# Inverting the triangular system of a gated delta rule: blocks of 32 solved on VectorE in place of blocks of 16 joined by products

## Chip, core and metric

The kernel runs on one core of a Trainium2 chip. The metric is the device time of one execution in microseconds (us). The core has TensorE (PE, with its weight loads shown as PEld), VectorE (DVE), ScalarE (ACT) and GpSimd (POOL); SyncE (SP) issues nearly all DMAs, in order, from one queue.

## The reference

The program is a whole small network on 256 tokens of width 1024: two layers of one kind (three sorts of attention), a norm, and then two layers of another kind (a mixer and a feed-forward). The change touches the mixer, and in it one branch, the chunked gated delta rule (4 heads, chunks of 64 tokens, key and value width 128). Cut to what matters:

```python
m = where(strict, einsum('bhnid,bhnjd->bhnij', k_beta, k) * decay, 0.0)
a = m + eye(64)                                    # unit lower triangular
rhs = concatenate([v * beta, k_beta * exp(G)])
u, w = split(triangular_solve(a, rhs))             # for each head and chunk
for each chunk:                                    # in order
    v_new = u - w @ state
    o     = q_dec @ state + attn @ v_new
    state = state * decay_last + k_tail.T @ v_new
```

Two tiles of 128 tokens hold four chunks; with 4 heads there are 8 matrices of 128x128, each with two triangular blocks of 64 on its diagonal. The mixer also has a retention branch, a pooling branch, gates, and three products (one for each branch) that are added up to `y`, which the output projection `w_out_2` takes.

## The kernel before

All large products are done as three fp32r products: weights are loaded from HBM as pieces of 128x1024 (512 KB) into `raw` (4 buffers); ACT casts a piece to `whi` and DVE subtracts to get `wlo` (7 buffers each); PE multiplies `whi` and `wlo` with the high and low parts of the activations (`xh`, `xl`) into `acc` (3 banks). Small products go to `sd` (5 banks) and are mostly plain fp32, which the trace shows as two records each.

The program is written down in one order, and each instruction is recorded with its inputs and outputs. A planner (`schedule`) then plays the five engines with estimated costs, always giving an engine the earliest recorded instruction that is ready, and hands out buffers of a class (`b` has 12 buffers of 4 KB per partition, `s` has 8) first come, first served in the order of the tiles. The order that comes out is what each engine executes. A dependency is seen by box: a slice of a rearranged view counts as the whole view, so two transfers into different slices of such a view follow one another in the plan.

In the mixer the inverse of each triangular block is built like this (`M` is the strict triangle, per tile `tt` and head `h`):

1. The products are masked to blocks of 16 (`m16`), and DVE folds each 128x128 to 128x16 (`tensor_reduce`, into `cN`, once for each `tt`). Eight transfers on SP's queue (8 KB each) bring one block to each of 64 partitions (`Nb`).
2. Substitution: 15 steps of two DVE instructions (a product into `tmp`, a subtraction from `Tb`) on 64 partitions, each step needing the one before. Step `j` has (15-j)(j+1) elements a partition.
3. Eight transfers bring the result back (`cT`), DVE spreads it to block diagonal form (`Tm`) and transposes it (`Sm`).
4. `level4` joins pairs of 16-blocks to 32-blocks: for each `tt` four PE products of `M` with `Sm`, a DVE mask (`mask4`), four PE products with `Tm`, a DVE subtraction from `Sm`, and DVE copies the 32-blocks to `Te`.
5. `level5` joins pairs of 32-blocks to 64-blocks with smaller products (recorded as 128*64 and 64*64).
6. `Sm` then gives `uu` and `wq`, and the loop over four chunks (the scan) runs through PE, ACT and DVE; its output `oTd` goes into the product with `w_branch_dn_2`, whose result is the last part of `y`.

The dense work that the text of the program puts around it, and that can fill PE while the chain of steps 1 to 6 waits, is: gate products, the branch products of pooling and retention, and the projections of v and q (`qkv`). The last dense work that does not need the scan's result is the two gate products `gate(0, h)`.

Of the kernel before, what the change touches and what calls it, by code (L numbers as in the profile page):

```python
# [13 lines left out]
ALU = mybir.AluOpType  # L14
# [29 lines left out]
def constants():  # L44
    t = np.arange(S)
    rc, rs = rope_np(t // 64, 32)
    cc, cs = rope_np(t % 64, 32)
    cosA, sinA = np.concatenate([rc, cc], 1), np.concatenate([rs, cs], 1)
    cosB, sinB = rope_np(t, 64)
    cosC, sinC = rope_np(t, 32)  # L50
    i = np.arange(P)
    ident = np.eye(P)
    m0 = np.where(i[None, :] <= i[:, None], 0.0, -1e30)
    mT0 = np.where(i[None, :] >= i[:, None], 0.0, -1e30)
    c1 = [ident, tok(cosA), tok(sinA), tok(cosB), tok(sinB), tok(cosC), tok(sinC), m0, mT0]
    same = (i[:, None] // 64) == (i[None, :] // 64)
    lt1 = (same & (i[:, None] <= i[None, :])).astype(float)
    ls = (same & (i[:, None] > i[None, :])).astype(float)
    r0 = np.repeat((i[:, None] < 64).astype(float), P, 1)
    r1 = 1.0 - r0  # L60
    masks = [((i[:, None] // 16) == (i[None, :] // 16)).astype(float)]
    for lv in range(4, 5):
        b = 2 ** lv
        masks.append((((i[:, None] // (2 * b)) == (i[None, :] // (2 * b)))
                      & ((i[None, :] // b) % 2 == 1) & ((i[:, None] // b) % 2 == 0)).astype(float))
    cosR, sinR = rope_np(t, 128)
    eye16 = np.tile(np.eye(16).reshape(1, 256), (P, 1))
    c2 = [lt1, ls, r0, r1, lt1.T] + masks + [tok(cosR), tok(sinR), eye16]
    gam = 1.0 - 2.0 ** (-5.0 - np.arange(4))
    jj, ii = t[:, None], t[None, :]  # L70
    ex = np.where((jj // 64) == (ii // 64), np.abs(ii - jj), ii - jj)
    dd = [np.where((jj // 64) <= (ii // 64), g ** np.maximum(ex, 0).astype(float), 0.0) * 128 ** -0.5 for g in gam]
    pc = []
    for w in (2, 4, 8, 16):
        pc.append(((jj <= ii) & (jj > ii - w)) / np.minimum(ii + 1.0, w) - (jj == ii))
    d0 = np.concatenate([a[:P] for a in dd], 1)
    d1 = np.concatenate([a[P:, P:] for a in dd], 1)
    p0 = np.concatenate([a[:P, :P + 16] for a in pc], 1)
    p1 = np.concatenate([a[P:, P:] for a in pc], 1)
    f = lambda l: np.ascontiguousarray(np.concatenate(l, 1).astype(np.float32))  # L80
    return {"k1": f(c1), "k2": f(c2), "kd0": f([d0]), "kd1": f([d1]), "kp0": f([p0]), "kp1": f([p1])}
# [313 lines left out]
class Net:  # L395
# [524 lines left out]


    def setup2(self):
        k2 = self.const("kk", [P, 1664], self.I["k2"])
        m = lambda i: k2[:, i * P:i * P + P]
        self.lt1, self.ls, self.r0, self.r1, self.li, self.m16 = (m(i) for i in range(6))
        self.mask4 = m(6)
        self.cosR = k2[:, 896:1152].rearrange("p (t d) -> p t d", t=2)
        self.sinR = k2[:, 1152:1408].rearrange("p (t d) -> p t d", t=2)
        self.eye16 = k2[:, 1408:1664].rearrange("p (r c) -> p r c", r=16)
        self.ones = self.nc.tile("c", [P, P])  # L930
        self.nc.vector.memset(self.ones, 1.0)
        self.lt1r = self.nc.tile("c", [P, P], F32R)
        self.nc.scalar.copy(self.lt1r, self.lt1)
# [4 lines left out]
    def mixer(self, l, xT, rx, nxt):  # L938
# [269 lines left out]

        y = [self.b(12 + tt, [P, D]) for tt in range(2)]
        branch("w_branch_pool_2", 0, oT, 0, gate(1, 0), True)  # L1210
        cp = self.b(0, [P, 832])
        cN, cT = (cp[:, i * P:i * P + P].rearrange("p (t h c) -> p t h c", t=2, h=4) for i in range(2))
        Nb, Tb = (cp[0:64, 320 + i * 256:576 + i * 256].rearrange("p (r c) -> p r c", r=16) for i in range(2))
        for tt in range(2):
            d16 = self.s2([P, 4, P])
            nc.vector.tensor_tensor(d16, M[:, tt], self.hb(self.m16), ALU.mult)
            nc.vector.tensor_reduce(cN[:, tt], d16.rearrange("p h (b c) -> p h c b", c=16), AX.X, ALU.add)
            for h in range(4):
                nc.sync.dma_start(Nb[(tt * 4 + h) * 8:(tt * 4 + h) * 8 + 8], cN[:, tt, h])
        nc.vector.tensor_copy(Tb, self.eye16[0:64])  # L1220
        for j in range(15):
            r, c = 15 - j, j + 1
            tmp = cp[0:64, 256:256 + r * c].rearrange("p (r c) -> p r c", r=r)
            nc.vector.tensor_tensor(tmp, Nb[:, c:16, j:j + 1].to_broadcast([64, r, c]),
                                    Tb[:, j:j + 1, 0:c].to_broadcast([64, r, c]), ALU.mult)
            nc.vector.tensor_tensor(Tb[:, c:16, 0:c], Tb[:, c:16, 0:c], tmp, ALU.subtract)
        for tt in range(2):
            for h in range(4):
                nc.sync.dma_start(cT[:, tt, h], Tb[(tt * 4 + h) * 8:(tt * 4 + h) * 8 + 8])
        Tm, Sm = self.b(8, [P, 2, 4, P]), self.b(9, [P, 2, 4, P])  # L1230
        for tt in range(2):
            nc.vector.tensor_tensor(Tm[:, tt].rearrange("p h (b c) -> p h b c", c=16),
                                    cT[:, tt].unsqueeze(2).to_broadcast([P, 4, 8, 16]),
                                    self.m16.rearrange("p (b c) -> p b c", c=16).unsqueeze(1).to_broadcast([P, 4, 8, 16]),
                                    ALU.mult)
            nc.vector.transpose(Sm[:, tt].rearrange("p h d -> p (h d)"), Tm[:, tt].rearrange("p h d -> p (h d)"))

        Te = [self.s2([64, 4, 64]) for tt in range(2)]

        def level4():  # L1240
            for tt in range(2):
                ps = self.sd([P, 4, P])
                for h in range(4):
                    nc.tensor.matmul(ps[:, h], M[:, tt, h], Sm[:, tt, h], start=True, stop=True)
                wt = self.s2([P, 4, P])
                nc.vector.tensor_tensor(wt, ps, self.hb(self.mask4), ALU.mult)
                ps = self.sd([P, 4, P])
                for h in range(4):
                    nc.tensor.matmul(ps[:, h], Tm[:, tt, h], wt[:, h], start=True, stop=True)
                nc.vector.tensor_tensor(Sm[:, tt], Sm[:, tt], ps, ALU.subtract)  # L1250
                for c in (0, 32):
                    nc.vector.transpose(Te[tt][c:c + 32, :, c:c + 32], Sm[2 * c:2 * c + 32, tt, :, 2 * c:2 * c + 32])
                    nc.gpsimd.memset(Te[tt][c:c + 32, :, 32 - c:64 - c], 0.0)

        def level5():
            v = lambda t: t.rearrange("p (c o r) -> p c o r", c=2, o=2)
# [22 lines left out]
        for tt in range(2):  # L1279
            nc.vector.tensor_tensor(kb[:, tt], kn[:, tt], hd(bGr, tt), ALU.mult)  # L1280
        branch("w_branch_ret_2", 0, oT, 4, gate(2, 0), False)
        level4()
        qkv(0, qT)
        rqs = []
        for tt in range(2):
# [219 lines left out]
```

## Time and profile before

| | us |
|---|---|
| median of 3 runs | 1184.65 (1184.16 to 1184.99) |
| profiled execution | 1186.84 |
| its span, first to last instruction | 1185.1 |
| PE busy in the span | 1167.3 |
| DVE busy | 875.3 |
| ACT busy | 651.0 |
| POOL busy | 48.2 |

Busy time is the union of an engine's instructions. The span is what the rows of the trace add up to; the profiled execution is 1.74 us longer than its span and 2.19 us longer than the median. The granted TensorE clock is 0.995 of full speed (2.4 GHz) over the span. Every instruction is recorded by one helper line (L392), so rows are told apart by engine, tile names and shapes. The two mixers are in the stretches around 200 to 520 us and 675 to 970 us.

### The profile page before, as it was taken

To read this page: it belongs to the slowest core of one execution; us is meant where nothing else is said; L and a number is where in the kernel's file an instruction comes from. 1 tells how busy PE (TensorE), PEld (TensorE's weight loads), DVE (VectorE), ACT (ScalarE), POOL (GpSimd) and SP (SyncE) were. 2 spreads that over 40 slices of the span, in tenths; PEclk is the share of its full clock that TensorE was granted. 3 is DMA by queue.
4 is the path that set the end of the run, shared out by engine and by line. 5 is a ranking of instruction groups with operands and counts; after the bars stand their busy time and mean duration, and the time that the engine had idled before them with its cause. 6 is when DMAs were issued, how large, how long until landed. Compare 5 with 4: busy or idle time off the path is not lost.

```text
span 1185.1 us, 17288 instructions
## 1 busy us (share of the span) xinstructions
PE 1167.3 (99%) x6316; PEld 989.9 (84%) x6316; DVE 875.3 (74%) x1549; ACT 651.0 (55%) x1209; POOL 48.2 (4%) x69
## 2 busy tenths in 40 slices
PE   8999999999999999999999999999999999999997
PEld 6888899888898888788888888898888878888886
DVE  5899789997698886776565638679797777655642
ACT  5689678965365554465454436445545446544531
POOL 0100010000001000000000001000000101000000
PEclk8999999999999999999999999999999999999999
DMA  6445345635464663345544854545654354654651
GB/s 235 137 145 167 122 130 175 194 128 174 119 212 144 210 203 128 103 160 198 209 156 136 273 194 142 170 141 169 220 186 152 107 178 140 202 192 142 214 195 36
DMA packets 64661, 196.67 MB, mean 166 GB/s; under 512 B 11200, under 2 KB 12352, under 8 KB 64576
## 3 DMA queue, kind: packets, MB, share of 16 engines
q1 hardware_dynamic: 64144, 195.10, 50.7%
q8 instruction: 49, 0.80, 0.3%
q10 hardware_dynamic: 432, 0.47, 0.1%
q14 instruction: 36, 0.29, 0.1%
HBM read 194.23 MB, written 1.05 MB: 165 GB/s over the span
## 4 chain that ended last, share of the span: by engine, by line
PE 92%; DVE 4%; ACT 2%; issue 1%; DMA 1%; ACTq 0%; POOLq 0%; DVEq 0%
PE acc L392 74%; PE sd L392 18%; DVE wlo L392 1%; DVE s L392 1%; DVE b L392 1%; DMA raw<-in_wt 1%; ACT whi L392 1%; ACT tg L392 0%; ACT s L392 0%; ACT b L392 0%; ACT xh L392 0%; DVE ty L392 0%; DVE m L392 0%; DVE tg L392 0%; DVE x L392 0%
## 5 line engine op out<-in xcount | busy, mean ns | idle before, releaser
L392 DVE TENSOR_TENSOR wlo<-raw,whi 128x1024 fp32r<-128x1024 f32 (+4 forms) x380 | 427.2, 1136 | 129.0 <-ACT whi L392 126.9
L392 ACT CAST whi<-raw 128x1024 fp32r<-128x1024 f32 (+4 forms) x379 | 368.2, 983 | 195.1 <-PE acc L392 140.7
L392 PE MATMUL acc<-whi,xh 128*128 128x512 f32 (+4 forms) x1184 | 446.1, 379 | 4.4 <-DVE ty L392 2.5
L392 PE MATMUL acc<-wlo,xh 128*128 128x512 f32 (+4 forms) x1184 | 442.9, 376 | 0.4 <-DVE wlo L392 0.4
L392 PE MATMUL acc<-whi,xl 128*128 128x512 f32 (+4 forms) x1184 | 442.9, 376 | 0.0
L392 PEld LDWEIGHTS acc<-whi,xh 128*128 128x128 f32 x1184 | 223.1, 189 | 42.7 <-ACT whi L392 3.3
L392 PEld LDWEIGHTS acc<-whi,xl 128*128 128x128 f32 x1184 | 223.5, 189 | 37.8 <-issue 0.4
L392 PEld LDWEIGHTS acc<-wlo,xh 128*128 128x128 f32 x1184 | 223.6, 189 | 37.7 <-DVE wlo L392 0.9
L392 PE MATMUL acc<-whi,b 128*128 128x512 f32 x328 | 107.4, 396 | 0.8 <-ACT b L392 0.8
L392 PEld LDWEIGHTS acc<-whi,b 128*128 128x128 f32 x328 | 61.5, 188 | 14.6 <-ACT b L392 1.1
L392 PE MATMUL sd<-b,b 128*128 128x128 f32 (+3 forms) x464 | 70.3, 289 | 0.0
L392 POOL TENSOR_TENSOR ty<-ty,m 128x4 f32<-128x4 f32 (+3 forms) x34 | 33.8, 997 | 886.3 <-DVE ty L392 886.3
L392 PE MATMUL acc<-wlo,b 128*128 128x512 f32 x164 | 64.5, 393 | 0.0
L392 PEld LDWEIGHTS sd<-b,b 128*128 128x128 f32 (+2 forms) x464 | 60.8, 190 | 4.3 <-DVE b L392 1.7
L392 ACT ACTIVATE b<-sd 128x512 fp32r<-128x512 f32 (+3 forms) x44 | 23.7, 538 | 64.7 <-PE sd L392 63.8
L392 ACT ACTIVATE s<-acc,r 128x512 f32<-128x512 f32 (+3 forms) x52 | 31.3, 601 | 49.1 <-PE acc L392 43.5
L392 PE MATMUL acc<-xh,wlo 128*128 128x256 f32 x192 | 53.9, 281 | 0.0
L392 PE MATMUL acc<-xh,whi 128*128 128x256 f32 x192 | 53.9, 281 | 0.0
L392 PE MATMUL acc<-xl,whi 128*128 128x256 f32 x192 | 53.8, 280 | 0.0
L392 DVE SCALAR_TENSOR_TENSOR b<-sd,b 128x512 fp32r<-128x512 f32 (+3 forms) x44 | 27.0, 616 | 18.7 <-ACT b L392 18.0
L392 PE MATMUL sd<-c,s 128*128 128x128 f32 (+2 forms) x236 | 36.7, 272 | 1.6 <-DVE s L392 1.6
L392 ACT ACTIVATE tg<-acc,r 128x512 f32<-128x512 f32 x24 | 16.5, 687 | 36.6 <-PE acc L392 36.6
(177 smaller groups left out, 1296.2 us busy)
## 6 DMA issues: line engine op xcount, KB each, us to landing
raw<-in_wt SPq DMA_DIRECT2D x308, 512.0 KB
raw<-in_wt SPq DMA_DIRECT2D x40, 256.0 KB
raw<-in_wt SPq DMA_DIRECT2D x16, 384.0 KB
b<-in_gains SPq DMA_DIRECT2D x5, 512.0 KB
raw<-in_wt SPq DMA_DIRECT2D x7, 352.0 KB
raw<-in_wt SPq DMA_DIRECT2D x8, 264.0 KB
b<-in_kd SPq DMA_DIRECT2D x2, 512.0 KB
kk<-in_k SPq DMA_DIRECT2D x1, 832.0 KB
```

The costliest lines, as they stand in the source:

```text
L392: o.inst = getattr(eng[o.eng], o.name)(*[real(a) for a in o.args], **{k: real(v) for k, v in o.kw.items()})
```

## The change

Masking, folding and substitution go by blocks of 32. The masks `m16` and `mask4` and the table `eye16` leave the constant `k2`, which shrinks from 1664 to 1280 columns; `m32` comes in. `cN` is 128x32 per tile and head. The eight transfers now bring 32-blocks to 32 partitions, into a tile `Nb` of its own, and are written with slices that are taken before any rearranging. The substitution is done in place in `Nb`, in 30 steps of two DVE instructions on 32 partitions; step `j` (1 to 30) has (31-j)j elements a partition. GpSimd writes -1 on the diagonals first. `level4` with its products goes. In its place `joined()`, recorded after the first half of the retention branch's product (where `level4` stood), negates `Nb` on ACT, sends it back in eight transfers, spreads it (`Tm`, now of class `s`), transposes it into `Sm`, and fills `Te` by four ACT copies. Tile `Sm` is asked for later than `vb` and `kb`, where it was before them; `Te` is asked for in `joined()`.

```diff
-        cp = self.b(0, [P, 832])
-        cN, cT = (cp[:, i * P:i * P + P].rearrange("p (t h c) -> p t h c", t=2, h=4) for i in range(2))
-        Nb, Tb = (cp[0:64, 320 + i * 256:576 + i * 256].rearrange("p (r c) -> p r c", r=16) for i in range(2))
+        cp = self.b(0, [P, 768])
+        cN, cT = (cp[:, i * S:i * S + S].rearrange("p (t h c) -> p t h c", t=2, h=4) for i in range(2))
+        Nb = self.b(0, [32, 32, 32])
         for tt in range(2):
-            d16 = self.s2([P, 4, P])
-            nc.vector.tensor_tensor(d16, M[:, tt], self.hb(self.m16), ALU.mult)
-            nc.vector.tensor_reduce(cN[:, tt], d16.rearrange("p h (b c) -> p h c b", c=16), AX.X, ALU.add)
-            for h in range(4):
-                nc.sync.dma_start(Nb[(tt * 4 + h) * 8:(tt * 4 + h) * 8 + 8], cN[:, tt, h])
-        nc.vector.tensor_copy(Tb, self.eye16[0:64])
-        for j in range(15):
-            r, c = 15 - j, j + 1
-            tmp = cp[0:64, 256:256 + r * c].rearrange("p (r c) -> p r c", r=r)
-            nc.vector.tensor_tensor(tmp, Nb[:, c:16, j:j + 1].to_broadcast([64, r, c]),
-                                    Tb[:, j:j + 1, 0:c].to_broadcast([64, r, c]), ALU.mult)
-            nc.vector.tensor_tensor(Tb[:, c:16, 0:c], Tb[:, c:16, 0:c], tmp, ALU.subtract)
-        for tt in range(2):
-            for h in range(4):
-                nc.sync.dma_start(cT[:, tt, h], Tb[(tt * 4 + h) * 8:(tt * 4 + h) * 8 + 8])
-        Tm, Sm = self.b(8, [P, 2, 4, P]), self.b(9, [P, 2, 4, P])
...
-        def level4():
+            d32 = self.s2([P, 4, P])
+            nc.vector.tensor_tensor(d32, M[:, tt], self.hb(self.m32), ALU.mult)
+            nc.vector.tensor_reduce(cN[:, tt], d32.rearrange("p h (b c) -> p h c b", c=32), AX.X, ALU.add)
+            for h in range(4):
+                nc.sync.dma_start(Nb[(tt * 4 + h) * 4:(tt * 4 + h) * 4 + 4], cp[:, (tt * 4 + h) * 32:(tt * 4 + h) * 32 + 32])
+        nc.gpsimd.memset(Nb.rearrange("p r c -> p (r c)")[:, 0:1024:33], -1.0)
+        for j in range(1, 31):
+            r, c = 31 - j, j + 1
+            tmp = cp[0:32, 512:512 + r * j].rearrange("p (r c) -> p r c", r=r)
+            nc.vector.tensor_tensor(tmp, Nb[:, c:32, j:c].to_broadcast([32, r, j]),
+                                    Nb[:, j:c, 0:j].to_broadcast([32, r, j]), ALU.mult)
+            nc.vector.tensor_tensor(Nb[:, c:32, 0:j], Nb[:, c:32, 0:j], tmp, ALU.subtract)
+        def joined():
+            nc.scalar.activation(Nb, Nb, AF.Copy, scale=-1.0)
             for tt in range(2):
-                ps = self.sd([P, 4, P])
                 for h in range(4):
-                    nc.tensor.matmul(ps[:, h], M[:, tt, h], Sm[:, tt, h], start=True, stop=True)
-                wt = self.s2([P, 4, P])
-                nc.vector.tensor_tensor(wt, ps, self.hb(self.mask4), ALU.mult)
-                ps = self.sd([P, 4, P])
-                for h in range(4):
-                    nc.tensor.matmul(ps[:, h], Tm[:, tt, h], wt[:, h], start=True, stop=True)
-                nc.vector.tensor_tensor(Sm[:, tt], Sm[:, tt], ps, ALU.subtract)
+                    nc.sync.dma_start(cp[:, S + (tt * 4 + h) * 32:S + (tt * 4 + h) * 32 + 32],
+                                      Nb[(tt * 4 + h) * 4:(tt * 4 + h) * 4 + 4])
+            Sm = self.b(9, [P, 2, 4, P])
+            Te = [self.s2([64, 4, 64]) for tt in range(2)]
+            for tt in range(2):
+                Tm = self.s2([P, 4, P])
...
+                nc.vector.transpose(Sm[:, tt].rearrange("p h d -> p (h d)"), Tm.rearrange("p h d -> p (h d)"))
                 for c in (0, 32):
-                    nc.vector.transpose(Te[tt][c:c + 32, :, c:c + 32], Sm[2 * c:2 * c + 32, tt, :, 2 * c:2 * c + 32])
+                    nc.scalar.copy(Te[tt][c:c + 32, :, c:c + 32], cT[2 * c:2 * c + 32, tt])
                     nc.gpsimd.memset(Te[tt][c:c + 32, :, 32 - c:64 - c], 0.0)
+            return Sm, Te
...
-        level4()
+        Sm, Te = joined()
```

## Rows read from the trace of the kernel before

**Rows 1.** The page: the span, and busy time, share and instructions of each engine

```profile
span 1185.1 us, 17288 instructions
PE 1167.3 (99%) x6316; PEld 989.9 (84%) x6316; DVE 875.3 (74%) x1549; ACT 651.0 (55%) x1209; POOL 48.2 (4%) x69
```

**Rows 2.** The page: the chain that ended last, shares of the span by engine

```profile
PE 92%; DVE 4%; ACT 2%; issue 1%; DMA 1%; ACTq 0%; POOLq 0%; DVEq 0%
```

**Rows 3.** Stretches: length, then busy us (instructions) of each engine, clock, DMA share, GB/s

```profile
376.00:389.50 13.50, 13.50 (x68) 11.30 (x67) 10.31 (x11) 7.10 (x8) 0.00 (x0) 1.00 0.70 210
389.50:426.00 36.50, 36.50 (x241) 33.14 (x240) 31.28 (x65) 17.62 (x22) 0.00 (x0) 1.00 0.65 214
426.00:441.00 15.00, 15.00 (x75) 12.54 (x74) 13.21 (x21) 9.40 (x15) 0.00 (x0) 1.00 0.55 161
441.00:454.00 13.00, 13.00 (x57) 10.53 (x56) 7.11 (x8) 4.83 (x6) 0.00 (x0) 1.00 0.63 203
470.00:490.00 20.00, 19.18 (x123) 16.26 (x122) 12.66 (x22) 8.87 (x21) 1.01 (x1) 1.00 0.41 132
490.00:520.00 30.00, 28.80 (x134) 23.05 (x135) 20.81 (x31) 12.49 (x24) 1.01 (x1) 1.00 0.48 158
903.00:916.00 13.00, 13.00 (x57) 10.50 (x57) 9.43 (x13) 4.89 (x5) 0.00 (x0) 1.00 0.60 191
950.00:1000.00 50.00, 49.25 (x231) 39.63 (x230) 38.20 (x70) 27.05 (x55) 4.14 (x5) 1.00 0.50 164
```

**Rows 4.** Timeline of PE, both mixers: start, length, operation, records, idle before

```profile
456.13 2.01 PE L392 MATMUL sd<-b,b 128*128 128x128 f32 x16
457.89 0.48 PE L392 MATMUL acc<-wlo,xh 128*128 128x512 f32 x1
...
458.64 1.95 PE L392 MATMUL sd<-s,b 128*128 128x128 f32 x16
460.43 0.60 PE L392 MATMUL sd<-c,b 128*128 128x128 f32 x4
...
462.75 0.68 PE L392 MATMUL sd<-b,s 128*64 128x64 f32 x8
...
489.87 0.50 PE L392 MATMUL acc<-whi,b 128*128 128x512 f32 x1 [0.82 <-ACT b L392]
```

**Rows 5.** Timeline of SP's queue: the small transfers (b<-b)

```profile
376.34 0.80 SPq L392 DMA_DIRECT2D b<-b  x1
...
387.35 0.61 SPq L392 DMA_DIRECT2D b<-b  x1
...
401.81 0.61 SPq L392 DMA_DIRECT2D b<-b  x1
...
447.99 0.63 SPq L392 DMA_DIRECT2D b<-b  x1
...
909.54 0.63 SPq L392 DMA_DIRECT2D b<-b  x1
```

**Rows 6.** Timeline of DVE in the two mixers

```profile
391.04 1.05 DVE L392 TENSOR_REDUCE b<-s 128x64 f32<-128x512 f32 x1
...
406.66 0.59 DVE L392 TENSOR_TENSOR b<-b 64x15 f32<-64x15 f32 x3
...
414.82 0.21 DVE L392 TENSOR_TENSOR b<-b 64x60 f32<-64x60 f32 x1
414.95 0.68 DVE L392 TENSOR_TENSOR b<-b,tg 128x512 f32<-128x512 f32 x1
...
421.83 1.80 DVE L392 TENSOR_TENSOR b<-b 64x55 f32<-64x55 f32 x8
...
454.12 1.29 DVE L392 TENSOR_TENSOR b<-b,kk 128x512 f32<-128x512 f32 x2
455.32 1.30 DVE L392 STREAM_TRANSPOSE b<-b 128x512 f32<-128x512 f32 x2
...
913.13 0.69 DVE L392 TENSOR_TENSOR b<-b,kk 128x512 f32<-128x512 f32 x1 [2.79 <-DMA raw<-in_wt]
```

**Rows 7.** Groups by shape: count, busy us, mean ns of one, idle before

```profile
L392 DVE TENSOR_TENSOR b<-b 64x63 f32<-64x63 f32 x8 | 1.7, 213 | 0.1
L392 DVE TENSOR_TENSOR b<-b 64x15 f32<-64x15 f32 x8 | 1.3, 168 | 0.2
L392 DVE STREAM_TRANSPOSE s<-b 32x128 f32<-32x128 f32 x8 | 2.4, 299 | 0.1
L392 ACT CAST whi<-raw 128x1024 fp32r<-128x1024 f32 x308 | 320.1, 1052 | 177.9 <-PE acc L392 124.4 <-DMA raw<-in_wt 22.8 <-PE sd L392 21.8
```

More of the change, by code (lines that the diff above doesn't have):

```diff
@@ L60, in constants @@
     r1 = 1.0 - r0
[L61 to L65, printed above, removed]
+    m32 = ((i[:, None] // 32) == (i[None, :] // 32)).astype(float)
     cosR, sinR = rope_np(t, 128)
-    eye16 = np.tile(np.eye(16).reshape(1, 256), (P, 1))
-    c2 = [lt1, ls, r0, r1, lt1.T] + masks + [tok(cosR), tok(sinR), eye16]
+    c2 = [lt1, ls, r0, r1, lt1.T, m32, tok(cosR), tok(sinR)]
     gam = 1.0 - 2.0 ** (-5.0 - np.arange(4))
@@ L922, in setup2 @@
     def setup2(self):
-        k2 = self.const("kk", [P, 1664], self.I["k2"])
+        k2 = self.const("kk", [P, 1280], self.I["k2"])
         m = lambda i: k2[:, i * P:i * P + P]
[L925 to L929, printed above, removed]
+        self.lt1, self.ls, self.r0, self.r1, self.li, self.m32 = (m(i) for i in range(6))
+        self.cosR = k2[:, 768:1024].rearrange("p (t d) -> p t d", t=2)
+        self.sinR = k2[:, 1024:1280].rearrange("p (t d) -> p t d", t=2)
         self.ones = self.nc.tile("c", [P, P])
@@ L1227, in mixer @@
-        for tt in range(2):
-            for h in range(4):
-                nc.sync.dma_start(cT[:, tt, h], Tb[(tt * 4 + h) * 8:(tt * 4 + h) * 8 + 8])
-        Tm, Sm = self.b(8, [P, 2, 4, P]), self.b(9, [P, 2, 4, P])
[L1231 to L1236, printed above, removed]
@@ L1238, in mixer @@
-        Te = [self.s2([64, 4, 64]) for tt in range(2)]
-        def level4():
+                nc.sync.dma_start(Nb[(tt * 4 + h) * 4:(tt * 4 + h) * 4 + 4], cp[:, (tt * 4 + h) * 32:(tt * 4 + h) * 32 + 32])
[6 more added lines that the diff above has]
+            nc.vector.tensor_tensor(Nb[:, c:32, 0:j], Nb[:, c:32, 0:j], tmp, ALU.subtract)
@@ L1250, in level4 @@
-                nc.vector.tensor_tensor(Sm[:, tt], Sm[:, tt], ps, ALU.subtract)
+                    nc.sync.dma_start(cp[:, S + (tt * 4 + h) * 32:S + (tt * 4 + h) * 32 + 32],
[4 more added lines that the diff above has]
+                Tm = self.s2([P, 4, P])
+                nc.vector.tensor_tensor(Tm.rearrange("p h (b c) -> p h b c", c=32),
+                                        cT[:, tt].unsqueeze(2).to_broadcast([P, 4, 4, 32]),
+                                        self.m32.rearrange("p (b c) -> p b c", c=32).unsqueeze(1).to_broadcast([P, 4, 4, 32]),
+                                        ALU.mult)
+                nc.vector.transpose(Sm[:, tt].rearrange("p h d -> p (h d)"), Tm.rearrange("p h d -> p (h d)"))
```

## The prediction

> **What bounds the kernel now.** I read the page first. PE is busy 1167.3 of 1185.1 us and holds 92% of the chain that ended last [rows 1, 2], so work taken from PE comes off the span if PE stays fed, and idle that the edit brings to PE goes on. Next I read the stretches around the edit. From 376 to 454 us PE has no idle at all, while DVE is busy 61.9 of 78 us, so DVE has 16.1 us to spare there [rows 3]. PE is idle 0.82 us in 470 to 490, 1.20 in 490 to 520, and in the second mixer 0.75 in 950 to 1000 [rows 3]. That small idle matters. The last timeline row of PE shows the first product of the branch that needs the scan (`acc<-whi,b`) starting at 489.87 after a wait for ACT's copy of the scan's result [rows 4]: the fillers ran out just as the scan ended. So two lines meet there, PE's total work and the chain from the fold of `M` through substitution, transfers, `level4`, `level5` and scan. A gain needs both to get shorter.
>
> The chain in the first mixer reads: first small transfer issued at 376.34, eighth at 401.81 [rows 5], substitution from 406.66 [rows 6] to about 425, last transfer back at 447.99 [rows 5], spreading at 454.12 and transposes from 455.32 [rows 6], `level4` on PE from 456.13, `level5` from 462.75 [rows 4]. From 455 on it is tight: the transposes of `Sm` and the first `level4` product overlap.
>
> **PE, the term of the sum.** `level4` is 16 fp32 products a mixer, 32 records. The first set holds PE from 456.13 to 457.89, 1.76 us; the second from 458.64 to 460.43, 1.79 us [rows 4]. That is 3.55 us a mixer, 7.1 us in all. Nothing is added on PE.
>
> **DVE.** The new substitution has 60 instructions in place of 30, with 2 x (sum of (31-j)j for j from 1 to 30) = 9920 elements in place of 1360. The rows give 168 ns for 15 elements and 213 for 63 [rows 7]: 0.94 ns an element. When another instruction follows, the next one starts 0.13 us after a product of 60 elements (414.82 to 414.95) [rows 6], so 0.074 us is fixed. When the chain runs alone, eight of mean 42.5 elements take 1.80 us [rows 6]: 0.225 each, 0.185 fixed. The new substitution therefore takes between 60 x 0.074 + 9.3 = 13.8 us and 60 x 0.185 + 9.3 = 20.4 us of DVE; the old one between 3.5 and 6.8. I expect some 40 of the 60 gaps of 0.11 us to be filled by other work, as in the rows of before, where products and casts alternate: 16 us. `level4` gives back two masks and two subtractions (0.6 us each from start to start) and four transposes of 0.30 us [rows 7]: 3.6 us. Net, DVE gets some 7 us a mixer; against 16.1 us to spare it fits, and the `wlo` casts stay covered because seven buffers are ahead of PE (ACT's casts wait mostly for PE to release one [rows 7]). Without that cover each late cast would stop PE for its lateness.
>
> Here a page of the Trainium skill speaks against the edit. VectorE: DVE Perf Modes (the section on the TRN2 errata) says that instructions from SBUF pay a fixed latency each, asks for 512 elements and more in one, and gives (N+151)/0.96 ns for an fp32 tensor_tensor. By it the 60 take 60 x 157 ns + 10.3 us = 19.8 us, as an estimate. The trace agrees with it for an instruction that stands alone (213 ns against 223 for 63 elements), not where another follows. By it the substitution would end near 450 and nearly nothing would be gained: the border between the first two rivals below.
>
> **The chain's new length.** I follow it in the first mixer.
> - Start. The first four transfers no longer follow one another: four issues of 0.62 us from 376.34. One landed 3.59 us after its issue began (909.54, and DVE's wait ends at 913.13) [rows 5, 6]. So `tt` 0 lands by 381.9. The second fold (1.05 us; it stood at 391.04, after the fourth transfer at 387.35) and four more transfers with two weight loads between them follow; the -1 on the diagonal is one short GpSimd instruction. Substitution starts near 389.5 instead of 406.66.
> - Substitution. From 389.5 to 426 DVE has 5.2 us idle [rows 3], plus the old substitution's 3.5 to 5.9 us and the old fold's 1.05: about 11 of the 16 to 16.4 us. The rest, about 20 instructions of 0.27 us, alternates with other instructions of 0.63 us (13.21 us for 21 [rows 3]): 18 us more, end at 444. Bounds: 436 if every gap is filled, 451 if none is.
> - Back. ACT's copy of 32x1024 costs at most the 1.05 us of a 128x1024 cast [rows 7], with a short wait 445.3. Eight issues of 0.62 us with two weight loads between: last issue near 450.3, landed at 453.9. Two spreads and two transposes, with `kb` ahead of them because `Sm` gets its buffer after it: `level5` can start near 457, bounds 449 and 464. It stood at 462.75.
>
> Two new waits have work queued behind them. DVE's first substitution step and its spreading wait for transfers, with `wlo` casts behind; at 910 to 913 DVE waited 2.79 us for such a transfer [rows 6] and PE had no idle from 903 to 916 [rows 3], so the seven prepared buffers cover that much. On SP's queue the eight returns wait for ACT's copy, with weight loads behind, as they waited for DVE's last step before; the same buffers cover it.
>
> The four ACT copies into `Te` (0.3 us each) lie in a stretch where ACT is busy 4.83 of 13 us [rows 3], and GpSimd is idle; both cost nothing. They would sit on the chain if they came after the transposes, at most 1.2 us. The shorter constant is 192 KB less once, at a time when PE is never short of weights: nothing.
>
> **The meeting point.** PE is 3.55 us ahead of before when `level4` is gone, so the whole gain needs `level5` at or ahead of 459.2 (substitution done by about 446); at 462.75 (substitution done by about 450) nothing is gained; later it costs. My 457 is inside by some 2 us. Then the scan ends 5.7 us earlier while PE is 3.55 earlier, so 2 us of fillers are left and part of the idle of 2.0 and 0.75 us goes too; I take 1 us of 2.75, because the waits at the end of the branch remain. Sum: 7.1 + 1.0 = 8.1 us. The profiled execution, 1186.84 us with span 1185.1, would become 1178.7, its span 1177; the median stands 2.19 us lower than the profiled execution, 1184.65, and becomes 1176.5.
>
> **Rivals.**
> - *DVE holds the substitution back.* Place: 389 to 450 us, where the substitution shares DVE with conv taps and `wlo`. For it: from 389.5 to 441 DVE is already 86% busy (44.5 of 51.5) [rows 3], and the chain cannot be hidden behind itself. Against: the substitution is recorded ahead of that work and so goes first whenever it is ready. It decides from an end at 450 on. At 451 and `level5` at 464 it costs 1.3 us a mixer past before, 1187; with 5 us more delay, 1197. Chance 13% of a loss over 0.2%.
> - *Part of the gain.* Substitution ends between 446 and 450; 0 to 7.1 us are left, 1178 to 1184. Chance 25%, 10 points of it within 0.2%.
> - *The transfers get slower.* They carry 128 pieces of 128 B where they had 64 B. If all of the 3 us between issue and landing doubled at the three places in the chain, `level5` comes 9 us later, at 466: 1184.65 + 2 x 3 = 1191. No row separates the time of the pieces from the fixed part. A rule of the Trainium skill makes it possible: DMA: Bandwidth & Descriptors (the section on why a DMA increments its semaphore by 16) has a transfer split over the largest number of engines that divides both slowest dimensions, which would be 4 here and was 8. No row here shows the engines of one transfer. Chance 4%, counted as slower by half.
> - *PE not the bound after all*, so that 3.55 us turn to waits elsewhere at once: 1184.65. Against: 92% of the chain is PE [rows 2]. Chance 3%.
>
> **Chances and range.** The full gain (1174.5 to 1178) has 55%; part of it, but over 0.2%, 15%; within 0.2% (2.4 us, about what a measurement of this kernel can tell from no change) 15%; slower 15%. The range reaches from 1174 (7.1 + 2.75 + the rounding of a record or two) to 1184.5, leaving out the losses and a few points of luck below. The likeliest case's own range is 1174.5 to 1178.
>
> **What would show it.** PE's records of `sd<-s,b 128x128` vanish and `sd<-b,b 128x128` fall by 32; PE's busy time falls by about 7 us and its idle does not grow. DVE shows 60 instructions on 32 partitions a mixer, from about 390 to 444, busy total up by some 14 us. The small transfers stand in groups of four and eight. `level5` (128*64) starts near 457 in the first mixer, with no PE wait ahead of it. I am wrong if PE shows idle of several us between 440 and 500 or `acc` products waiting for `wlo`; then the substitution's last instruction after 450 names the DVE rival, a long wait of the spreading instruction for a transfer the other.

## The result, and the profile after

| | before | after |
|---|---|---|
| median, both on one chip | 1184.82 us (1184.16 to 1186.09, 4 runs) | 1172.74 us (1172.02 to 1173.72, 4 runs) |
| profiled execution, its span | 1186.84, 1185.1 | 1172.4, 1170.6 |

The ratio is 0.9897, 95% interval 0.988 to 0.9914: the change gains 12.1 us where 8.1 were forecast, and 1172.74 lies 1.3 us below the range of 1174.0 to 1184.5. The sign was right, the size was not.

The page of the kernel after, its first lines (span, busy time of each engine) and the shares of the chain that ended last, which answer to [rows 1] and [rows 2]:

```profile
span 1170.6 us, 17214 instructions
PE 1155.2 (99%) x6252; PEld 980.1 (84%) x6252; DVE 886.7 (76%) x1591; ACT 653.5 (56%) x1219; POOL 49.3 (4%) x71
...
PE 85%; DVE 8%; ACT 3%; issue 2%; DMA 1%; SPq 1%; POOLq 0%; DVEq 0%; ACTq 0%
```

PE is busy 12.1 us less and its idle falls from 17.8 to 15.4 us (span less busy). That the 12.1 equals the gain of the medians is chance: 2.5 us of it lie ahead of the first mixer, for the reason below, and 9.6 behind. DVE does 11.4 us more. The chain's share of PE fell from 92 to 85%, and yet PE is idle less: the view follows one way back, and where two lines are both just in time it may as well take the one through DVE. The idle in the stretches, not the share, says what bounds.

The two profiled executions differ by 14.4 us, the medians by 12.1. The difference is in the beginning, which the change touches only by a smaller constant. Stretches of the kernel after and, below it, of the kernel before (columns as in [rows 3]):

```profile
20.00:40.00 20.00, 18.77 (x96) 15.06 (x97) 17.76 (x42) 12.77 (x27) 2.91 (x2) 1.00 0.53 158
```

```profile
20.00:40.00 20.00, 18.42 (x85) 14.40 (x84) 16.12 (x36) 13.30 (x27) 3.14 (x3) 0.91 0.47 145
```

The granted clock was 0.91 in these 20 us before, 1.00 after, and with it PE reaches the gate math of the first mixer (the products `sd<-m,kk`) at 346.39 before and 343.99 after. So the times of after that follow are 2.4 us early against those of before; the rows show no other reason, and all ten traces fit it (last section). From that mark to the same mark of the second mixer it is 461.55 us before and 454.75 after, from there to the end of the span 377.16 and 371.86: 6.8 and 5.3 us, together the 12.1.

The chain in the first mixer, after. SP's queue with the small transfers (`b<-b`), answering to [rows 5]:

```profile
373.65 2.57 SPq L387 DMA_DIRECT2D b<-b  x4
376.32 2.15 SPq L387 DMA_DIRECT2D raw<-in_wt  x4
379.14 2.47 SPq L387 DMA_DIRECT2D b<-b  x4
382.51 50.64 SPq L387 DMA_DIRECT2D raw<-in_wt  x17
435.30 5.21 SPq L387 DMA_DIRECT2D b<-b  x8
```

DVE's timeline, answering to [rows 6]:

```profile
378.03 1.08 DVE L387 TENSOR_REDUCE b<-s 128x128 f32<-128x512 f32 x1
...
386.86 0.19 DVE L387 TENSOR_TENSOR b<-b 32x30 f32<-32x30 f32 x1
387.08 0.20 DVE L387 TENSOR_TENSOR b<-b,b 32x30 f32<-32x30 f32 x1
...
402.24 0.47 DVE L387 SCALAR_TENSOR_TENSOR s<-s,pp,s 128x255 f32<-128x255 f32 x1
402.63 0.38 DVE L387 TENSOR_TENSOR b<-b,b 32x228 f32<-32x228 f32 x1
402.94 0.47 DVE L387 SCALAR_TENSOR_TENSOR s<-s,pp,s 128x255 f32<-128x255 f32 x1
403.33 0.38 DVE L387 TENSOR_TENSOR b<-b 32x234 f32<-32x234 f32 x1
...
433.96 0.17 DVE L387 TENSOR_TENSOR b<-b,b 32x30 f32<-32x30 f32 x1
...
442.80 1.29 DVE L387 TENSOR_TENSOR b<-b,m 128x512 f32<-128x512 f32 x2 [1.19 <-DMA b<-b]
444.01 1.29 DVE L387 TENSOR_TENSOR s<-b,kk 128x512 f32<-128x512 f32 x2
```

PE's timeline around `level5`, answering to [rows 4]:

```profile
433.86 0.60 PE L387 MATMUL sd<-c,b 128*128 128x128 f32 x4
...
446.61 1.15 PE L387 MATMUL sd<-b,s 128*64 128x64 f32 x16
...
449.20 1.11 PE L387 MATMUL sd<-s,s 64*64 64x64 f32 x16 [0.31 <-ACT s L387]
```

The stretches of [rows 3], shifted by 2.7 us; the columns are the same:

```profile
386.80:423.30 36.50, 36.50 (x242) 33.08 (x241) 36.02 (x80) 15.48 (x19) 0.00 (x0) 1.00 0.51 158
423.30:438.30 15.00, 15.00 (x82) 12.69 (x81) 14.96 (x36) 9.91 (x14) 0.00 (x0) 1.00 0.53 171
438.30:451.30 13.00, 12.69 (x84) 10.26 (x83) 10.79 (x24) 8.54 (x29) 1.98 (x2) 1.00 0.47 151
467.30:487.30 20.00, 20.00 (x101) 16.42 (x100) 16.47 (x24) 11.02 (x20) 2.02 (x2) 1.00 0.55 179
```

What to see: four transfers are issued in a row and no longer follow one another; substitution runs from 386.86 to 434.13, between `wlo` casts and conv taps (`s<-s,pp,s`), with DVE busy 36.02 of 36.50 us and then 14.96 of 15.00; PE does not notice, it has no idle until 438. The spreading (`s<-b,kk`) is at 444.01, and `level5` starts at 446.61 with no wait ahead of it, 102.6 us after the mark, where it was 116.4 before; a short wait of 0.31 us comes behind it. Around the end of the scan, where PE was idle 0.82 us before, it has no idle now. By shape, `sd<-b,b 128x128` has 208 records in place of 240 and `sd<-s,b`, 32 records before, is gone.

Both PE timelines, each product's time taken from its start to the start of the next, give the 12.1 us in three parts (idle is the waits of 0.15 us and more):

| | from the first mark to the second | from there to the end | sum | forecast |
|---|---|---|---|---|
| products of `level4` | 3.56 | 3.56 | 7.1 | 7.1 |
| PE idle | 1.70 | 0.65 | 2.35 | 1.0 |
| all other products, a little closer together | 1.5 | 1.1 | 2.6 | 0 |

The idle of before that matters lies in four waits around the end of the scan: the one at 489.87 [rows 4], here with the group ahead of it, and three more. The second fence is of after, where no wait is left at this place:

```profile
488.45 0.60 PE L392 MATMUL sd<-c,b 128*128 128x128 f32 x4
...
496.44 0.66 PE L392 MATMUL sd<-c,b 128*128 128x128 f32 x4 [0.35 <-DVE b L392]
497.95 0.47 PE L392 MATMUL acc<-whi,xh 128*128 128x512 f32 x1 [0.85 <-DVE tg L392]
...
957.98 0.47 PE L392 MATMUL acc<-whi,xh 128*128 128x512 f32 x1 [0.75 <-ACT b L392]
```

```profile
494.62 0.60 PE L387 MATMUL sd<-c,b 128*128 128x128 f32 x4
494.97 0.48 PE L387 MATMUL acc<-whi,xh 128*128 128x512 f32 x1
```

A wait costs more than the idle that the row names. Before, four records start at 488.45 and the next product at 489.87, 1.42 us later, of which 0.82 are idle; after, the next product starts 0.35 us behind the start of such a group. The wait of 0.82 us thus cost 1.07, because the last product ahead of a wait stands with its whole length and otherwise overlaps the next. The four waits, 2.77 us of idle, have about 0.25 us each of this, 1.0 us in all, and it stands in the third row of the table.

### The profile page after: what moved, and what is told of

It reads as the page before. It is cut to its first block, busy times and chain, and to the rows that moved or that the text cites. A ratio compares the mean times of both kernels' runs of the same rounds, so it can differ in the third digit from the quotient of the medians.

```text
span 1170.6 us, 17214 instructions
## 1 busy us (share of the span) xinstructions
PE 1155.2 (99%) x6252; PEld 980.1 (84%) x6252; DVE 886.7 (76%) x1591; ACT 653.5 (56%) x1219; POOL 49.3 (4%) x71
## 4 chain that ended last, share of the span: by engine, by line
PE 85%; DVE 8%; ACT 3%; issue 2%; DMA 1%; SPq 1%; POOLq 0%; DVEq 0%; ACTq 0%
PE acc L387 68%; PE sd L387 17%; DVE b L387 3%; DVE wlo L387 2%; DVE s L387 2%; DMA raw<-in_wt 1%; ACT whi L387 1%; ACT s L387 1%; ACT tg L387 1%; SPq L387 1%; DMA b<-b 0%; ACT b L387 0%; ACT xh L387 0%; DVE ty L387 0%; DVE xl L387 0%
## 5 line engine op out<-in xcount | busy, mean ns | idle before, releaser
L387 PE MATMUL sd<-b,b 128*128 128x128 f32 (+4 forms) x432 | 66.8, 290 | 0.0
L387 PEld LDWEIGHTS sd<-b,b 128*128 128x128 f32 (+2 forms) x432 | 57.1, 190 | 4.1 <-DVE b L387 1.3
```

The source lines that it names most:

```text
L387: o.inst = getattr(eng[o.eng], o.name)(*[real(a) for a in o.args], **{k: real(v) for k, v in o.kw.items()})
```

## The experiments

**The theory.** PE and the chain are two lines that meet at `level5` and at the end of the scan; the gain is PE's products plus the idle that the chain no longer causes, and after the change the chain has time to spare. Rivals: the transfers alone did it; the products did it alone and DVE's part is idle luck; or the chain is still what sets the end. Costs below are against the kernel after, from the difference of the two ratios times the 1184.65 us of before. "From the mark on" compares the traces behind the first mixer's `sd<-m,kk`, where the beginning no longer plays a part.

**The transfers alone.** The kernel before with slices taken ahead of any rearranging:

```diff
-                nc.sync.dma_start(Nb[(tt * 4 + h) * 8:(tt * 4 + h) * 8 + 8], cN[:, tt, h])
+                i = tt * 4 + h
+                nc.sync.dma_start(cp[i * 8:i * 8 + 8, 320:576].rearrange("p (r c) -> p r c", r=16), cp[:, i * 16:i * 16 + 16])
...
-                nc.sync.dma_start(cT[:, tt, h], Tb[(tt * 4 + h) * 8:(tt * 4 + h) * 8 + 8])
+                i = tt * 4 + h
+                nc.sync.dma_start(cp[:, P + i * 16:P + i * 16 + 16], cp[i * 8:i * 8 + 8, 576:832].rearrange("p (r c) -> p r c", r=16))
```

> The kernel before with one part of the change alone: the sixteen small transfers are written with slices taken before any rearranging, so the plan no longer sets them one behind the other. Blocks stay at 16, level4 and its products stay. Theory A (two lines: PE's work, and the chain that meets it at the end of the scan): the chain starts some 17 us earlier, PE's work is unchanged; what goes is PE's idle at the end of the scan (1.7 us in the first mixer, 0.65 in the second by the two traces) and the hidden waits of the small products (about 2.2 us in both): 1184.8 - 2.4 - (0 to 2.2) = 1180 to 1182.5. Theory B (the whole gain is work taken from PE): 1184.8, within 0.1%. Theory C (the chain's start, not the products, brought most of the 12 us): 1177 or lower.

Measured: 1181.67 us, ratio 0.9968 [0.9957, 0.998], 3.8 us off before. PE's timeline of this kernel, the first product of `level5`:

```profile
438.24 0.68 PE L392 MATMUL sd<-b,s 128*64 128x64 f32 x8
```

It stood at 462.75; against the mark it comes 22.3 us earlier. A chain so much shorter, with the same products on PE, is worth little more than the idle around the scan (2.75 us in the rows of before): PE's total then decides. From the mark on, the trace is 3.4 us shorter than that of before: 2.5 us of idle and the rest mostly what hung on the four waits. Theory A holds.

**The transfers undone.** The kernel after, with whole rearranged views as before:

```diff
-        Nb = self.b(0, [32, 32, 32])
+        Nb = self.b(0, [32, 1024]).rearrange("p (r c) -> p r c", r=32)
...
-                nc.sync.dma_start(Nb[(tt * 4 + h) * 4:(tt * 4 + h) * 4 + 4], cp[:, (tt * 4 + h) * 32:(tt * 4 + h) * 32 + 32])
+                nc.sync.dma_start(Nb[(tt * 4 + h) * 4:(tt * 4 + h) * 4 + 4], cN[:, tt, h])
...
-                    nc.sync.dma_start(cp[:, S + (tt * 4 + h) * 32:S + (tt * 4 + h) * 32 + 32],
+                    nc.sync.dma_start(cT[:, tt, h],
```

> The changed kernel with the small transfers written through rearranged views again, so that the plan sets them one behind the other; blocks of 32, no level4. Theory A: the fold of the second tile and the substitution start some 17 us later and the way back is some 15 us longer; level5, which stands at 449 on the clock of the trace before, moves to about 480, against 462.75 before; some 17 us a mixer late less 7 us of PE's lead is exposed, as far as no dense work can be pulled forward: 1172.7 + 2 x (10 to 20) = 1190 to 1212. Theory B: 1172.7, since PE's work is the same; up to 1176 with some idle. The rival of the prediction that DVE holds the chain back has the same sign as A here and is told apart by the run that doubles DVE's products.

Measured: 1226.17 us, ratio 1.0342 [1.0328, 1.0356]: 53 us over after and 3.4% slower than before. PE's timeline, `level5` in both mixers:

```profile
480.94 1.97 PE L387 MATMUL sd<-b,s 128*64 128x64 f32 x16 [12.12 <-DVE b L387]
...
963.54 1.97 PE L387 MATMUL sd<-b,s 128*64 128x64 f32 x16 [12.05 <-DVE b L387]
```

The same sixteen transfers a mixer that were worth 3.8 us with the short substitution are worth 53 with the long one, since most of the delay now lies past the chain's spare (see the detours below). The sign was expected, the size not: the waits of 12.1 us are only about half. The stretch that begins before the first of them shows the rest:

```profile
470.00:490.00 20.00, 9.06 (x56) 8.83 (x57) 7.79 (x14) 5.29 (x11) 0.52 (x1) 0.58 0.34 111
490.00:520.00 30.00, 23.99 (x118) 19.72 (x117) 14.93 (x29) 7.16 (x23) 2.02 (x2) 0.77 0.11 36
```

PE is busy 9.06 of 20 us and the granted clock is 0.58, so nearly all of this stretch is at the lower of the two levels, 1.2 GHz, and a part of the next 30 us still is. The 16 records of `level5` take 1.97 us where they take 1.15 after. From the mark of the first mixer to that of the second, idle grew by 17.8 us and the products, the same in number, took 9.8 us more from start to start.

**The products put back.** The kernel after, with as many products as `level4` had, in a block ahead of `joined()`; nothing reads their results:

```diff
+        for tt in range(2):
+            for n in range(2):
+                ps = self.sd([P, 4, P])
+                for h in range(4):
+                    nc.tensor.matmul(ps[:, h], M[:, tt, h], M[:, tt, h], start=True, stop=True)
         Sm, Te = joined()
```

> The changed kernel with 16 fp32 products of 128x128 a mixer (M with M, results read by nobody) recorded ahead of the joining step: PE's work of before without level4's place in the chain. Theory A: the price of the products alone, 7.1 us by the rows of before (7.6 by the difference of the two traces): 1172.7 + 7.1 to 7.6 = 1179.8 to 1180.4, with PE's idle as small as in the changed kernel. Theory B (all 12 us are the products and what hangs on them on PE): 1183 to 1185. Theory C: the products fill idle of PE, under 3 us: below 1175.7.

Measured: 1183.36 us, ratio 0.9988 [0.9977, 0.9999], 10.8 us over after, more than the products' own time and in theory B's interval. PE's timeline:

```profile
414.05 3.73 PE L387 MATMUL sd<-b 128*128 128x128 f32 x32
...
445.91 0.68 PE L387 MATMUL sd<-b,s 128*64 128x64 f32 x8 [0.62 <-ACT s L387]
```

The records take 3.5 us a mixer from start to start, 7.0 together. From the mark on the trace is 10.3 us longer than that of after: these 7.0, 1.6 of new idle (most of it at `level5`, which now waits 0.62 and 0.99 us for ACT) and 1.7 in other products, 0.5 of them because `level5` runs as groups of 8 again. So the number falls in theory B's interval, but a third of it is not the products: it is waits and spacing that came with this plan.

**The same products, spread.** To see whether the block makes it dear, the same 16 were placed one at a time between the steps of a dense product (pooling, second half):

```diff
             self.mm3(ps, xh[:, k0 + k, s], xl[:, k0 + k, s], wh[:, k % KT], wl[:, k % KT], k == 0, k == nk - 1)
+            if getattr(self, "extra", None) and k < nk - 1:
+                self.extra.pop()()
...
+        def product(tt, h):
+            ps = self.sd([P, P])
+            nc.tensor.matmul(ps, M[:, tt, h], M[:, tt, h], start=True, stop=True)
+        self.extra = [lambda tt=tt, h=h: product(tt, h) for n in range(2) for tt in range(2) for h in range(4)]
         branch("w_branch_pool_2", 1, oT, 0, gate(1, 1), True)
```

> The changed kernel with 16 extra fp32 products a mixer, as in the run that had them in one block, now one at a time between the dense fp32r products of the gate and pooling branch. The block cost 10.6 us where its own records took 7.0. Theory A (a small fp32 group inside the dense stream costs more than its own records, 0.09 us and up for each return to dense products): some 13 more insertions a mixer cost 26 x 0.09 to 0.2 = 2.3 to 5.2 us on the products' own 7.1: 1182 to 1185. Theory B (insertions cost nothing; the block's 3.5 us extra were waits that it brought to the small products behind it): 1179.8 to 1180.5.

Measured: 1183.84 us (1180.59 to 1184.96, 12 runs), ratio 0.999 [0.998, 1.0]: 11 us over after, the same as the block. That the number falls in theory A's interval does not bear out its account, since spreading changed nothing, and theory B's lower figure was missed too. The profiled execution is 8.2 us over that of after, but it began with the clock at 1.00 and reached the mark 1.3 us sooner; from the mark on it is 9.5 us longer. Of these 4.9 are the products' records from start to start and 2.6 the dense product behind each insertion (0.32 us in place of 0.23), together 7.5 where the block took 7.0; 1.1 are new idle (0.91 and 0.74 us at `level5`, for ACT again) and the rest is spacing. So an insertion costs about 0.1 us, but its records take less (0.08 us each, 0.11 in the block), and spreading changes little.

**The chain later by one detour.** In `joined()`, a quarter of `Nb` makes a way out and back by two transfers that follow one another:

```diff
         def joined():
+            for n in range(1):
+                t = cp[0:32, 512:768].rearrange("p (r c) -> p r c", r=8)
+                nc.sync.dma_start(t, Nb[:, 0:8])
+                nc.sync.dma_start(Nb[:, 0:8], t)
             nc.scalar.activation(Nb, Nb, AF.Copy, scale=-1.0)
```

> The changed kernel with one detour in the chain: after the substitution a quarter of Nb is sent to a scratch area and back by two transfers that follow one another, some 7 us of waiting with no work on PE or DVE. Theory A: level5 goes from 449 to about 456 on the clock of the trace before; PE's line, which has lost 7 us of work and idle, would need it by 462.75 - 6.9 = 455.9: 1172.7 to 1174.7. Theory B (chain hidden): 1172.7. Theory C (chain binds in the changed kernel): 1172.7 + 2 x 7 = 1186.7.

Measured: 1173.04 us, ratio 0.9894 [0.9881, 0.9908]. `level5` came 6.5 us later in the first mixer and 7.2 in the second, both against the mark, and the time did not move. In the first mixer that is 455.5 on the clock of before, close to the 457 that the prediction had, and of the four waits around the scan only one of 0.25 us is there.

**By two detours.** The same with `range(2)`.

> The changed kernel with two detours in the chain (four transfers one behind the other after the substitution), some 14 us of waiting with no work on PE or DVE. One detour moved level5 from 449 to 456 on the clock of the trace before and cost nothing. Theory A (the chain has some 7 us to spare and then binds): level5 near 463, 7 us past the point where PE's line needs it; dense work pulled forward hides a part: 1172.7 + 2 x (1.5 to 7) = 1176 to 1187. Theory B (the chain is hidden whatever its length, and the boxed run lost its time elsewhere): 1172.7 to 1174.

Measured: 1188.54 us, ratio 1.0027 [1.0016, 1.0038]: 15.4 us over after, and 1.5 above theory A's interval. PE's timeline of the first mixer, with one detour and then with two:

```profile
453.24 0.68 PE L387 MATMUL sd<-b,s 128*64 128x64 f32 x8
```

```profile
459.92 0.68 PE L387 MATMUL sd<-b,s 128*64 128x64 f32 x8
...
463.65 0.65 PE L387 MATMUL sd<-s,s 64*64 64x64 f32 x8 [1.59 <-ACT s L387]
...
485.31 1.16 PE L387 MATMUL sd<-st,b 128*128 128x128 f32 x8 [2.15 <-DVE st L387]
```

Now `level5` is 14.4 and 15.0 us later than after and PE has waits at each step of the chain behind it. The first 7 us were free, the next 7 to 8 cost 15.4 in both mixers together, about one to one if the spare ends at 7, which no run shows more closely than between 7 and 14. It is an average: from the first mark to the second this trace is 11.4 us longer than that of after, from there to the end 3.4. In the first mixer the waits brought the clock down:

```profile
466.00:470.00 4.00, 4.00 (x23) 4.00 (x23) 0.00 (x0) 0.96 (x2) 0.00 (x0) 0.57 0.27 102
470.00:486.00 16.00, 13.18 (x86) 11.05 (x85) 11.81 (x18) 7.98 (x17) 2.05 (x1) 1.00 0.55 169
486.00:494.00 8.00, 6.97 (x27) 5.78 (x26) 4.24 (x9) 2.19 (x9) 0.68 (x1) 0.57 0.15 58
```

There the products took 6.1 us more beside 5.3 of idle; in the second mixer, where the clock stayed at 1.00, only 0.7 more. The twelve executions took from 1184.4 to 1190.2 us, and this trace is of one 2.4 us below the median. The run with whole views fits the average too: there `level5` is 32.7 and 35.1 us later, 25.7 and 28.1 past a spare of 7, together 53.8, and 53 were measured. Theory B falls here, and with one detour the rival by which the chain still sets the end in the kernel after.

**The substitution's DVE work.** Its product is done twice, into the same `tmp`:

```diff
+            nc.vector.tensor_tensor(tmp, Nb[:, c:32, j:c].to_broadcast([32, r, j]),
+                                    Nb[:, j:c, 0:j].to_broadcast([32, r, j]), ALU.mult)
             nc.vector.tensor_tensor(Nb[:, c:32, 0:j], Nb[:, c:32, 0:j], tmp, ALU.subtract)
```

> The changed kernel with each product of the substitution done twice into the same scratch (30 more DVE instructions a mixer, same results): 6.9 to 10.2 us more DVE work in the chain and in the stretch where DVE is fullest. Theory A (only the chain's end counts, and it has 7 us to spare): level5 comes 7 to 10 us later, 456 to 459 on the clock of the trace before: 1172.7 to 1178. The prediction's rival (DVE short of time, so that wlo casts come late and PE starves): over 1180, with PE's dense products waiting for wlo in the trace.

Measured: 1201.68 us, ratio 1.014 [1.0126, 1.0154]: 28.8 us over after for 30 short instructions a mixer. Theory A falls for this step, the DVE rival came. DVE's timeline (the last instruction of the substitution), PE's, and the stretches:

```profile
456.83 0.18 DVE L387 TENSOR_TENSOR b<-b,b 32x30 f32<-32x30 f32 x1
```

```profile
447.62 0.50 PE L387 MATMUL acc<-whi,xh 128*128 128x512 f32 x1 [2.21 <-DVE tg L387]
...
451.35 0.79 PE L387 MATMUL acc<-wlo,xh 128*128 128x512 f32 x1 [3.23 <-DVE wlo L387]
...
469.75 0.68 PE L387 MATMUL sd<-b,s 128*64 128x64 f32 x8
```

```profile
390.00:426.00 36.00, 36.00 (x235) 32.52 (x234) 35.56 (x78) 14.98 (x20) 0.00 (x0) 1.00 0.51 163
426.00:441.00 15.00, 14.88 (x77) 12.14 (x76) 15.00 (x37) 9.21 (x20) 0.00 (x0) 1.00 0.36 113
441.00:454.00 13.00, 7.56 (x27) 5.57 (x26) 11.84 (x30) 3.55 (x13) 1.98 (x2) 0.78 0.27 92
```

DVE was full already, so 30 more instructions end the substitution 22.9 us later and push `wlo` and the retention's `tg` behind them; PE, whose cover lasted to 441, then waits for both, and the clock of that stretch is 0.78. `level5` is 23.2 and 24.2 us later than after. Of PE's waits over 0.3 us in the chain's stretch of both mixers, 8.2 us are for `tg` and `wlo`, ahead of `level5`, and 7.3 for the chain behind it. Both mechanisms are there, and the run does not separate their costs.

**The products and masks of `level4` taken away.** The kernel before without the products, masks and subtractions of `level4`; pairs of 16-blocks are not joined, so that part of the inverse is left out.

```diff
-                ps = self.sd([P, 4, P])
-                for h in range(4):
-                    nc.tensor.matmul(ps[:, h], M[:, tt, h], Sm[:, tt, h], start=True, stop=True)
-                wt = self.s2([P, 4, P])
-                nc.vector.tensor_tensor(wt, ps, self.hb(self.mask4), ALU.mult)
-                ps = self.sd([P, 4, P])
-                for h in range(4):
-                    nc.tensor.matmul(ps[:, h], Tm[:, tt, h], wt[:, h], start=True, stop=True)
-                nc.vector.tensor_tensor(Sm[:, tt], Sm[:, tt], ps, ALU.subtract)
```

> The kernel before with level4's products, masks and subtractions left out (16-blocks are not joined to 32-blocks; the copies into Te stay): its output is not the reference's. Transfers stay one behind the other in the plan. Theory A (PE's line 3.8 us shorter a mixer, chain 6.6 us shorter because level4's time goes): both lines get shorter by more than PE's part, so products 7.1 to 7.6 and part of the idle of 2.4: 1184.8 - 7.1 to 10 = 1175 to 1178. Theory B (chain binds in before and only its length counts): 1184.8 - 2 x 6.6 = 1171.6. Theory C (without the earlier chain the products' removal turns into idle): 1181 or more.

Measured: 1174.83 us, ratio 0.9916 [0.9902, 0.9929], 10.0 us off before, at the fast end of theory A's interval; B and C fall. This is not the products alone, since `level5` also comes 10.2 and 8.7 us earlier against the mark: from the mark on, the trace is 10.2 us shorter, 7.1 for the records of `level4`, 2.0 of idle and 1.1 in other products. `level4` taken away gives 10.0, the transfers alone 3.8, both 12.1: less than the sum, since the idle around the scan can be given back only once. No run takes the products off PE and leaves the chain as long as it was.

## Why the prediction was off, point by point

- **PE is the bound (92% of the chain, no idle from 376 to 454): right.** Taking `level4` away gave 10.0 us, more than its records' 7.1. The rival in which PE is not the bound falls.
- **The products, 7.1 us: right.** The sets of the second mixer, from start to start, are 1.78 and 1.78 us beside the 1.76 and 1.79 of the first.
- **The meeting point: right in kind.** A shorter chain alone was worth 3.8 us, `level4` taken away 10.0, a chain 7 us later nothing, one 15 us later 15.4. The deadline for `level5` was put at 459.2 on the clock of before, 112.8 us after the mark; by the detours it lies between 109.1, which cost nothing, and 117.1, which did, so the forecast is neither refuted nor shown.
- **The sum is where it failed: "I take 1 us of 2.75, because the waits at the end of the branch remain. Sum: 7.1 + 1.0 = 8.1 us."** Those waits did not remain: all four, 2.77 us, are gone, and with the 0.31 us that came in at `level5` and smaller differences 2.35 us of idle went. It was not only that the chain came out shorter than forecast: with one detour `level5` stood at 455.5, near my 457, and only one wait of 0.25 us came back. And the 2.6 us by which all other products moved closer together stood in the sum at nothing, in the range at "a record or two". Of these, 1.0 us is what the same four waits cost beyond their idle, and it went with the transfers alone too, so it goes with the chain and not with the products. The 16 records of `level5`'s first product run as one group of 1.15 us, where two groups of 8 took 0.68 each [rows 4]; with the 64*64 products that is 0.5 us over both mixers, but it depends on the plan, since with one detour they are two groups again. The 16 records `sd<-b,b` ahead of `level5` before (1.88 us a mixer) are two groups of 0.81 after, 0.5 us in all. The last 0.6 are open. So the waits at the scan were worth 3.4 us in all, not 1.0, as the run with the transfers alone (3.8) says by itself.
- **The chain's steps**, on the clock of before (after plus 2.4): start of the substitution 389.3 for a forecast of 389.5; its end 436.5 for 444 with 436 to 451 as bounds; `level5` 449.0 for 457 with 449 to 464. Start and bounds were right, the middle was too late. The 60 instructions took 16.0 us from start to start, as I had said; 47 of them had another instruction behind them, where I had counted 40. What was too high was the other work between: by the end of the stretch at 423.3 on the clock of after, 46 were done and not 40, and the last 14 alternated with 14 others of 0.60 us, 10.8 us in place of 18. (The old substitution stands in that sum with 3.5 to 5.9 us, where I had found 3.5 to 6.8 a few lines before.) The transfers back took 5.21 us for eight, without weight loads between, in place of some 5 with them.
- **DVE, net 7 us a mixer: 5.7** (11.4 over the whole). The rule of the Trainium skill that I weighed (VectorE: DVE Perf Modes, TRN2 errata) would have ended the substitution near 450. The trace agrees with it for instructions that stand alone and not for these. The rows of after show the difference: the 32x228 product lasts 0.38 us, and the next instruction, on other data, starts 0.31 us after its start, so a part of the fixed time is overlapped.
- **The DVE rival (13%)** did not come, and its mechanism is real: 30 more instructions a mixer brought its marks, `acc` products waiting for `wlo` among them, at 28.8 us together with a later chain.
- **Slower transfers (4%)**: no sign. Issues are 0.62 to 0.65 us each as before, and the substitution started when forecast. The landing of 3.59 us that I used is weakly founded, since its row names a weight transfer (`raw<-in_wt`) as what ended the wait. After, DVE's wait for the eight returns ends at 442.80, 2.3 us after the last issue ended at 440.51; and the two transfers of a detour, one behind the other, put in 6.5 to 7.2 us.

Faster, to which I gave 70%, came; the range was too narrow at its fast end. It did take in both whole idles, 2.75. What it lacked is what a wait costs beyond its idle (1.0 us) and the groups that closed up (1.0 us and 0.6 unexplained), where it allowed 0.8.

## What to carry to other kernels

Where two lines meet, cost both before and after: work taken off the bounding engine counts in full if the other line has slack left, which a deliberate delay (7 us a mixer cost nothing, 15 us cost 15.4 over two mixers) shows better here than the view of the chain. Read a wait's price from start to start, not from its idle alone (1.07 us for 0.82 here). A long chain of small dependent instructions can be nearly free while other instructions fill its gaps (60 here, no idle on PE), and very dear from the point where its engine is full (30 more, 28.8 us), so look at that engine's busy time in the stretch and not over the span. Where a planner sees dependencies by whole views, write the slices so that independent transfers look independent: here worth 3.8 us with the short substitution and 53 with the long one.

## What the hardware showed that I had not expected

- A late chain costs more than the waits that the profile names. Where PE had waited, the granted clock was low: 0.58 and 0.77 in the two stretches of the run with whole views, 0.78 in that with the doubled product, 0.57 twice in the first mixer with two detours. In the run with whole views, idle made 17.8 us of the cost of the first mixer and slower products 9.8. With two detours nearly the same lateness cost 11.4 us in the mixer where the clock fell and 3.4 in the one where it did not.
- The granted clock of the first 40 us differs from trace to trace. The mark of the first mixer comes at 342.7 to 343.0 us in the three traces with 1.00 in 0 to 20 and in 20 to 40 us, at 343.9 to 344.2 in the five with 0.91 in one of them, and at 345.7 and 346.4 where it is 0.83 in one or 0.91 in both (before). Over whole executions it is the same: of the 23 of before on the second chip, the five with a mean clock of 0.999 took 1182.9 to 1183.6 us, the eight with 0.997 took 1183.9 to 1184.3, the ten with 0.995 or 0.996 took 1185.8 to 1186.4. At 0.997 these have a median of 1184.2, and the two executions of after at 0.997 took 1172.4 and 1173.1: a gain of some 11.4 us, a little less than the 12.1 of the medians, if the chips are alike.
